# A planner that charges no lag between two operations of one stream on one engine

## The chip, the core and the metric

The kernel runs on one core of one Trainium2 chip. The metric is device time in microseconds (us) of one execution of the whole program. The core has five engines that read their own instruction queues in order: TensorE (PE in the profile; PEld is its weight load), VectorE (DVE), ScalarE (ACT), GpSimd (POOL) and SyncE (SP), which issues most of the transfers.

## The reference, cut to what matters

One encoder block on 256 tokens of width 2048, in float32. One input projection feeds two branches, latent attention and a two-way RWKV-7 scan; both are gated, projected, merged, projected again, normalised and added to the input.

```python
h = rms_norm(x, g_pre)
proj = h @ w_in                      # 2048 x 10688
mla_in, rwkv_in, z_mla, z_rwkv, gate_mla, gate_rwkv = jnp.split(proj, ...)
q = rms_norm(q_a) @ mla_wq_b;  kv = rms_norm(kv_a) @ mla_wkv_b
y_mla = mla_attention(q_nope, rot(q_rope), k_nope, rot(k_rope), v_mla)   # 8 heads, softmax
rin = rin + rwkv_mu * (centred_shift(rin) - rin)
w, a = decay(...), sigmoid(...)      # low-rank, forward and backward
# for each of 256 steps, both directions, 16 heads of 64 x 64:
#   st = st * w_t + (st @ a_t) b_t^T + v_t k_t^T ;  y_t = st @ r_t
y = rwkv7_bidir_scan(r_h, hd(w_f), hd(w_b), k_fh, k_bh, v_h, kk, hd(a_f), hd(a_b))
y_rwkv = group_norm(y) + bonus * v
u_mla  = (y_mla  * silu(z_mla))  @ w_br_mla
u_rwkv = (y_rwkv * silu(z_rwkv)) @ w_br_rwkv
merged = sigmoid(gate_mla) * u_mla + sigmoid(gate_rwkv) * u_rwkv
x = x + rms_norm(merged @ w_out, g_post)
```

## The kernel before, in words

**The main line.** All large products run on PE as three matmuls each: every float32 operand is split into a high part and the rest (hi and lo), and hi x hi, hi x lo and lo x hi are summed in PSUM. The weights come in 249 chunks, most of 512 KB. A chunk is loaded by SyncE into one of three `raw` buffers, ACT writes its high part to one of three `whi` (line 327, reached from the split stream), DVE writes the rest to one of three `wlo` (L330), and PE consumes it: four steps of six matmuls of 256 columns in the input projection (L396 and L397 read `whi`, L398 reads `wlo`). So a split can start only when PE has finished the chunk three places ahead of it, and PE stands still when the next `wlo` is late.

**The side work.** The RWKV heads are handled in four quads of four heads. For each quad: the operands are prepared (`front_k`, `front_v`, `front_d`, `bonus`); PE makes eight groups of Gram products and transposes (L797, L805), which DVE masks out of PSUM into `g` (five banks go round); DVE turns part of them by two long transposes (L818, L819) and inverts 32 x 32 triangles in place, 30 rounds of a multiply into `tmp` and an add into `u` (both at helper line L191), each of which needs the one before it. Then four scan steps alternate between PE (L892 or L912 with L914, then L923, then L941 with L944) and copies on ACT and DVE (L916 and L918, L925 and L927), and a group norm ends the quad (`yr`). This side work has no priority in time of its own; what PE does in between is the main line.

**What sets the order.** The program is written out by a planner, the class `Streams`, while the kernel is built. Every piece of work is a generator (a stream) that asks for an engine (P, A, D, G or S for PE, ACT, DVE, GpSimd, SyncE) with a cost in us and, where it names one, a ready time. After each pick the stream's own time `s[2]` is set to the end of that operation plus `LAG` of the engine: 0.25 us for P, 0.12 for A, D and G, 2.0 for S. The next request of the stream is ready at that time unless it names another. On each engine the planner takes, among requests that could start within `SLOT` (0.08 us on DVE, 0.06 on ACT, 0.03 on PE) of the earliest, the one with the lowest rank. The main matmuls have rank 9. The stream that splits chunks has rank 1 when fewer than two chunks are split ahead of the matmuls, and otherwise 8. The quads' chain (`chunks_of`) has rank 2, `front_k` and `front_d` 3, `bonus` 5, the evictions of Gram products 0. The planner's times are its own and do not reach the chip: only the order of each engine's instructions and their semaphore waits do.

Of the kernel before, what the change touches and what calls it, by code (L numbers as in the profile page):

```python
# [43 lines left out]
class Streams:  # L44
# [11 lines left out]
        self.mode = "128x128"  # L56

    def add(self, gen, rank, t=0.0):
        s = [gen, rank, t, None]
        self.live.append(s)  # L60
        self._next(s, None)
        return s
# [15 lines left out]
    def run(self, until=None):  # L78
        while self.live and not (until and until()):
            moved = True  # L80
            while moved:
                moved = False
                for s in list(self.live):
                    while s in self.live and s[3][0] in "WT" and (s[3][0] == "T" or s[3][1]()):
                        if s[3][0] == "T":
                            s[2] = max(s[2], s[3][1])
                        self._next(s, s[2])
                        moved = True
            if until and until():
                return  # L90
            ask = {}
            for i, s in enumerate(self.live):
                q = s[3]
                if q[0] != "W":
                    ready = s[2] if len(q) < 3 or q[2] is None else q[2]
                    rank = s[1]() if callable(s[1]) else s[1]
                    ask.setdefault(q[0], []).append((max(self.free[q[0]], ready), rank, i, s))
            best = None
            for e, c in ask.items():
                first = min(c)[0] + SLOT[e]  # L100
                start, _, _, s = min((x for x in c if x[0] <= first), key=lambda x: (x[1], x[0], x[2]))
                if best is None or start < best[2]:
                    best = (e, s, start)
            if best is None:
                if not self.live:
                    return
                raise RuntimeError("every stream waits: " + " ".join(self.where(x[0]) for x in self.live))
            _, s, start = best
            e, cost = s[3][0], s[3][1]
            if e == "P":  # L110

                mode = s[3][3] if len(s[3]) > 3 else "128x128"
                cost += 0.2 * (mode != self.mode)
                self.mode = mode
            elif len(s[3]) > 3 and s[3][3] != self.table:
                self.table = s[3][3]
                cost += 1.3
            self.free[e] = start + cost
            self.used[e] += cost
            s[2] = start + cost + self.LAG[e]  # L120
            self._next(s, s[2])
# [1532 lines left out]
```

## Time and profile before

| what | us |
|---|---|
| three timed runs: median, lowest, highest | 875.97, 873.17, 876.22 |
| profiled execution, its own time | 872.72 |
| its span, first to last instruction | 870.9 |
| PE busy (8112 matmuls) | 848.3 |
| DVE busy | 659.3 |
| ACT busy | 501.1 |

The span is 1.8 us shorter than the execution's own time. A matmul's record is longer than its place in the row: records of 0.28 us follow each other every 0.12 us, so that a busy PE is not a PE at its peak, and an idle gap of PE is shown shorter than it is. In a row of the timeline, the bracket at the end gives how long the engine was idle before it and which instruction released it. Names such as `wlo`, `g`, `u`, `yr` are tiles, with the buffer number left out.

### The profile page before, as it was taken

To read this page: it belongs to the slowest core of one execution; us is meant where nothing else is said; L and a number is where in the kernel's file an instruction comes from. 1 tells how busy PE (TensorE), PEld (TensorE's weight loads), DVE (VectorE), ACT (ScalarE), POOL (GpSimd) and SP (SyncE) were. 2 spreads that over 40 slices of the span, in tenths; PEclk is the share of its full clock that TensorE was granted. 3 is DMA by queue.
4 is the path that set the end of the run, shared out by engine and by line. 5 is a ranking of instruction groups with operands and counts; after the bars stand their busy time and mean duration, and the time that the engine had idled before them with its cause. 6 is when DMAs were issued, how large, how long until landed. Compare 5 with 4: busy or idle time off the path is not lost.

```text
span 870.9 us, 19398 instructions
## 1 busy us (share of the span) xinstructions
PE 848.3 (97%) x8112; PEld 810.0 (93%) x8112; DVE 659.3 (76%) x1082; ACT 501.1 (58%) x797; POOL 30.7 (4%) x66
## 2 busy tenths in 40 slices
PE   9999999999999999999999999999999999999996
PEld 8999999988899998999889999899999999998884
DVE  5878898868987878988789878775867556775554
ACT  6777644487544578354776445586766434444442
POOL 4110000000000000000000000000000000000000
PEclk9999999999999999999999999999999999999999
DMA  9565646633376523565423665346444675555553
GB/s 286 169 181 148 176 129 187 169 99 90 101 212 177 161 68 97 158 193 169 132 76 96 195 188 152 98 149 186 136 128 147 232 257 190 176 193 193 194 195 119
DMA packets 123528, 139.41 MB, mean 160 GB/s; under 512 B 6704, under 2 KB 110512, under 8 KB 123056
## 3 DMA queue, kind: packets, MB, share of 16 engines
q1 hardware_dynamic: 121664, 135.16, 52.4%
q0 software_dynamic: 768, 1.57, 0.6%
q10 hardware_dynamic: 1008, 1.44, 0.5%
q8 instruction: 63, 1.03, 0.5%
q14 instruction: 25, 0.20, 0.1%
HBM read 136.05 MB, written 2.10 MB: 159 GB/s over the span
## 4 chain that ended last, share of the span: by engine, by line
PE 73%; DVE 14%; ACT 8%; issue 2%; DMA 2%; DVEq 0%; ACTq 0%
PE d L396 16%; PE d L398 16%; PE d L397 15%; DVE wlo L330 4%; PE m L1334 2%; PE m L1335 2%; PE m L1336 2%; ACT whi L327 2%; DVE work L191 2%; PE m L398 2%; PE m L396 2%; PE m L397 2%; PE d L1335 1%; PE d L1334 1%; PE d L1336 1%
## 5 line engine op out<-in xcount | busy, mean ns | idle before, releaser
L327 ACT CAST whi<-raw 128x1024 fp32r<-128x1024 f32 (+3 forms) x252 | 252.8, 1004 | 254.2 <-PE d L397 155.1
L330 DVE TENSOR_TENSOR wlo<-raw,whi 128x1024 fp32r<-128x1024 f32 (+3 forms) x250 | 292.4, 1171 | 125.0 <-ACT whi L327 123.4
L396 PE MATMUL d<-hhi,whi 128*128 128x256 f32 (+1 forms) x1296 | 375.1, 289 | 0.0
L398 PE MATMUL d<-hhi,wlo 128*128 128x256 f32 (+1 forms) x1296 | 366.5, 283 | 2.3 <-DVE wlo L330 2.3
L397 PE MATMUL d<-hlo,whi 128*128 128x256 f32 (+1 forms) x1296 | 366.2, 283 | 0.0
L396 PEld LDWEIGHTS d<-hhi,whi 128*128 128x128 f32 (+1 forms) x1296 | 246.8, 190 | 4.5
L398 PEld LDWEIGHTS d<-hhi,wlo 128*128 128x128 f32 (+1 forms) x1296 | 246.9, 190 | 2.7 <-DVE wlo L330 2.7
L397 PEld LDWEIGHTS d<-hlo,whi 128*128 128x128 f32 (+1 forms) x1296 | 247.1, 191 | 0.1
L191 DVE TENSOR_TENSOR work<-work,work 128x512 f32<-128x512 f32 (+5 forms) x64 | 38.8, 612 | 3.9 <-ACT work L575 1.2
L191 DVE TENSOR_TENSOR u<-u,tmp 128x30 f32<-128x30 f32 (+7 forms) x120 | 29.9, 250 | 3.0
L191 DVE TENSOR_TENSOR tmp<-u 128x30 f32<-128x30 f32 (+7 forms) x120 | 29.8, 249 | 2.9
L396 PE MATMUL d<-b,whi 128*128 128x256 f32 x96 | 27.1, 282 | 0.0
L398 PE MATMUL d<-b,wlo 128*128 128x256 f32 x96 | 27.1, 282 | 0.0
L398 PE MATMUL d<-ar,wlo 128*128 128x256 f32 x96 | 27.0, 281 | 0.0
L397 PE MATMUL d<-work,whi 128*128 128x256 f32 x96 | 26.9, 280 | 0.0
L397 PE MATMUL d<-ar,whi 128*128 128x256 f32 x96 | 26.9, 280 | 0.0
L396 PE MATMUL d<-ar,whi 128*128 128x256 f32 x96 | 26.8, 279 | 0.0
L1334 PE MATMUL m<-whi,hhi 128*128 128x512 f32 x60 | 23.3, 389 | 0.0
L1335 PE MATMUL m<-wlo,hhi 128*128 128x512 f32 x60 | 23.3, 389 | 0.0
L1336 PE MATMUL m<-whi,hlo 128*128 128x512 f32 x60 | 23.3, 389 | 0.0
L191 DVE TENSOR_TENSOR g<-m,mask 128x512 f32<-128x512 f32 x32 | 20.6, 686 | 0.0
L797 PE MATMUL m<-ar,u 64*128 64x128 f32 x256 | 19.2, 285 | 0.3 <-DVE g L191 0.3
(334 smaller groups left out, 1487.3 us busy)
## 6 DMA issues: line engine op xcount, KB each, us to landing
raw<-in_w_in_dram SPq DMA_DIRECT2D x160, 512.0 KB, 3.9
raw<-in_w_out_dram SPq DMA_DIRECT2D x32, 512.0 KB, 3.6
raw<-in_w_br_mla_dram SPq DMA_DIRECT2D x16, 512.0 KB, 4.0
raw<-in_w_br_rwkv_dram SPq DMA_DIRECT2D x16, 512.0 KB, 3.3
raw<-in_mla_wkv_b_dram SPq DMA_DIRECT2D x8, 512.0 KB, 3.9
raw<-in_mla_wq_b_dram SPq DMA_DIRECT2D x8, 384.0 KB, 3.3
raw<-in_w_in_dram SPq DMA_DIRECT2D x7, 384.0 KB, 5.3
g<-in_x_dram SPq DMA_DIRECT2D x2, 1024.0 KB, 6.9
```

What stands on the lines that cost most here:

```text
L191: dve.tensor_tensor(out=o, in0=a, in1=b, op=op)
L327: act.copy(dst(c.hi), src(raw))
L330: eng.tensor_tensor(out=dst(c.lo), in0=src(raw), in1=dst(c.hi).bitcast(F32), op=ALU.subtract)
L396: pe.matmul(o, hi[:, c:c + m], xhi(k), start=k == k_first and i % 2 == 0, stop=False)
L397: pe.matmul(o, hi[:, c:c + m], xlo(k), start=False, stop=False)
L398: pe.matmul(o, lo[:, c:c + m], xhi(k), start=False, stop=last)
L797: pe.matmul(m[:, q * 128:q * 128 + 128], z.kb[R64[h], d, j, q], z.ar[d][R64[h], j, q], start=q == 0, stop=q == 3)
L1334: pe.matmul(banks[t], hhi[:, k, T], hi, start=k == 0, stop=False)
L1335: pe.matmul(banks[t], hhi[:, k, T], lo, start=False, stop=False)
L1336: pe.matmul(banks[t], hlo[:, k, T], hi, start=False, stop=k == KT - 1)
```

## The change

A stream's record gets a fifth field, the engine of its last operation. When the stream's next request is for the same engine and its ready time is the stream's own time, the lag is taken off again: the planner then treats the next operation as ready the moment the last one ends, whether or not it reads what the last one wrote. A request for another engine keeps the lag. Nothing else is edited, and both programs hold the same instructions on every engine: 7026 on PE, 1080 on DVE, 778 on ACT by the builder's count; PE also changes between its tile shapes 140 times in each.

```diff
     def add(self, gen, rank, t=0.0):
-        s = [gen, rank, t, None]
+        s = [gen, rank, t, None, ""]
...
                 if q[0] != "W":
                     ready = s[2] if len(q) < 3 or q[2] is None else q[2]
+                    if s[4] == q[0] and ready == s[2]:
+
+                        ready -= self.LAG[q[0]]
                     rank = s[1]() if callable(s[1]) else s[1]
...
             _, s, start = best
             e, cost = s[3][0], s[3][1]
+            s[4] = e
```

What it moves is seen in the order of the instructions. Line numbers of the changed kernel are higher by 4.

DVE, first quad, start of the inversion (`tmp` and `u`), behind its second transpose; `wlo` rows are chunk splits, `work` rows with `qpad` or `d` evict a projection. Before:

```order
132 L330 TENSOR_TENSOR wlo_22_84<-raw_16_78,whi_19_81 128x1024
133 L191 TENSOR_TENSOR tmp_1365<-u_81_1364 128x30
134 L191 TENSOR_TENSOR u_81_1364<-u_81_1364,tmp_1365 128x30
135 L191 TENSOR_TENSOR tmp_1365<-u_81_1364 128x29
136 L330 TENSOR_TENSOR wlo_23_85<-raw_17_79,whi_20_82 128x1024
137 L191 TENSOR_TENSOR work_25_87<-qpad_51_121 128x512
138 L191 TENSOR_TENSOR u_81_1364<-u_81_1364,tmp_1365 128x29
139 L194 SCALAR_TENSOR_TENSOR work_28_90<-d_112,iv_66,work_25_87 128x256
140 L191 TENSOR_TENSOR tmp_1365<-u_81_1364 128x56
141 L194 SCALAR_TENSOR_TENSOR work_28_90<-d_112,iv_66,work_25_87 128x256
142 L191 TENSOR_TENSOR u_81_1364<-u_81_1364,tmp_1365 128x28x2
143 L330 TENSOR_TENSOR wlo_21_83<-raw_15_77,whi_18_80 128x1024
```

Now:

```order
127 L334 TENSOR_TENSOR wlo_23_85<-raw_17_79,whi_20_82 128x1024
128 L195 TENSOR_TENSOR tmp_1272<-u_81_1271 128x29
129 L195 TENSOR_TENSOR u_81_1271<-u_81_1271,tmp_1272 128x29
130 L195 TENSOR_TENSOR tmp_1272<-u_81_1271 128x56
131 L195 TENSOR_TENSOR u_81_1271<-u_81_1271,tmp_1272 128x28x2
132 L195 TENSOR_TENSOR tmp_1272<-u_81_1271 128x54
133 L195 TENSOR_TENSOR u_81_1271<-u_81_1271,tmp_1272 128x27x2
134 L195 TENSOR_TENSOR tmp_1272<-u_81_1271 128x78
135 L334 TENSOR_TENSOR wlo_21_83<-raw_15_77,whi_18_80 128x1024
136 L195 TENSOR_TENSOR u_81_1271<-u_81_1271,tmp_1272 128x26x3
```

Rounds of the inversion stand next to each other, seven instructions between two splits, where other work stood between them.

DVE, fourth quad, the end of the Gram products (`g`) and the two transposes; `yr` rows are the group norm of the third quad. Before:

```order
637 L330 TENSOR_TENSOR wlo_22_84<-raw_16_78,whi_19_81 128x1024
638 L191 TENSOR_TENSOR yr_113<-yr_113,work_196_5489 128x512
639 L191 TENSOR_TENSOR g_198_5523<-m_106,mask_63 128x512
640 L191 TENSOR_TENSOR g_198_5523<-m_105,mask_63 128x512
641 L194 SCALAR_TENSOR_TENSOR yr_113<-yr_113,iv_66,work_26_88 128x256 x2
642 L191 TENSOR_TENSOR yr_113<-yr_113,work_37_99 128x512
643 L818 STREAM_TRANSPOSE u_204_5657<-g_198_5523 32x1024
644 L819 STREAM_TRANSPOSE u_204_5657<-g_198_5523 32x1024
645 L330 TENSOR_TENSOR wlo_23_85<-raw_17_79,whi_20_82 128x1024
```

Now:

```order
623 L334 TENSOR_TENSOR wlo_23_85<-raw_17_79,whi_20_82 128x1024
624 L195 TENSOR_TENSOR g_198_5492<-m_108,mask_63 128x512
625 L195 TENSOR_TENSOR g_198_5492<-m_106,mask_63 128x512
626 L822 STREAM_TRANSPOSE u_204_5578<-g_198_5492 32x1024
627 L823 STREAM_TRANSPOSE u_204_5578<-g_198_5492 32x1024
628 L198 SCALAR_TENSOR_TENSOR work_25_87<-work_109_2439,d_110 128x512
629 L334 TENSOR_TENSOR wlo_21_83<-raw_15_77,whi_18_80 128x1024
```

The group norm of the quad before has moved ahead of this place, and one split stands right in front of the last two evictions.

PE, third quad, the first scan step: L892 opens it, L923 needs the copy of its result, and what stands between covers that copy (L684 to L686 are a low-rank product, L587 and L588 head sums). Before:

```order
3069 L892 MATMUL m_105<-uv_3970,g_157_4061 64x64 x8
3070 L684 MATMUL m_108<-tw_45_115,work_165_5000 128x256
3071 L685 MATMUL m_108<-tw_46_116,work_165_5000 128x256
...
3075 L686 MATMUL m_108<-tw_45_115,work_166_5001 128x256
3076 L923 MATMUL m_105<-work_161_4195,g_157_4061 64x64 x8
```

Now:

```order
2924 L896 MATMUL m_109<-uv_3775,g_157_4038 64x64 x8
2925 L688 MATMUL m_107<-tw_45_115,work_165_4834 128x256
...
2931 L591 MATMUL m_106<-work_167_4846,bdr_68 128x256
...
2935 L400 MATMUL d_111<-hhi_75,whi_19_81 128x256
...
2940 L402 MATMUL d_111<-hhi_75,wlo_22_84 128x256
2941 L927 MATMUL m_109<-work_61_806,g_157_4038 64x64 x8
```

Between the two, 6 matmuls stood before and 16 stand now.

## Rows read from the trace of the kernel before

**Rows 1.** Page, part 1: engines' busy us, share of the span, instructions.

```profile
PE 848.3 (97%) x8112; PEld 810.0 (93%) x8112; DVE 659.3 (76%) x1082; ACT 501.1 (58%) x797; POOL 30.7 (4%) x66
```

**Rows 2.** Timeline of PE, two matmuls of the main line: start, us, instruction.

```profile
239.15 0.28 PE L396 MATMUL d<-hhi,whi 128*128 128x256 f32 x1
239.27 0.28 PE L397 MATMUL d<-hlo,whi 128*128 128x256 f32 x1
```

**Rows 3.** Stretches: length; busy PE, PEld, DVE, ACT, POOL (instructions); clock, DMA share, GB/s.

```profile
90.00:150.00 60.00, 60.00 (x525) 58.97 (x524) 52.03 (x91) 29.65 (x39) 1.13 (x3) 1.00 0.58 162
210.00:240.00 30.00, 28.59 (x258) 26.96 (x256) 29.59 (x41) 20.84 (x31) 1.02 (x2) 1.00 0.34 96
450.00:480.00 30.00, 28.92 (x264) 27.50 (x262) 28.31 (x40) 22.07 (x34) 0.00 (x0) 1.00 0.32 89
```

**Rows 4.** Waits of PE: who, for whom: us in total, times, longest.

```profile
PE m L923 <- DVE work L918: 3.1, 8, 0.7
PE d L398 <- DVE wlo L330: 2.3, 2, 1.2
PE m L587 <- ACT work L435: 1.3, 2, 0.7
PE m L588 <- DVE work L191: 1.2, 5, 0.3
PE m L1414 <- POOL ones L250: 1.1, 1, 1.1
...
PE m L1203 <- ACT work L1194: 0.2, 1, 0.2
```

**Rows 5.** Timeline of DVE in the first quad's inversion.

```profile
120.51 0.21 DVE L191 TENSOR_TENSOR tmp<-u 128x30 f32<-128x30 f32 x1
120.75 0.21 DVE L191 TENSOR_TENSOR u<-u,tmp 128x30 f32<-128x30 f32 x1
...
123.30 0.21 DVE L191 TENSOR_TENSOR u<-u,tmp 128x29 f32<-128x29 f32 x1
123.42 0.48 DVE L194 SCALAR_TENSOR_TENSOR work<-d,iv,work 128x256 f32<-128x256 f32 x1
...
141.72 1.23 DVE L330 TENSOR_TENSOR wlo<-raw,whi 128x1024 fp32r<-128x1024 f32 x1 [0.49 <-ACT whi L327]
```

**Rows 6.** Waits of all engines, the two that hold the splits.

```profile
ACT whi L327 <- PE d L397: 155.1, 102, 2.2
DVE wlo L330 <- ACT whi L327: 123.4, 136, 5.5
```

**Rows 7.** Timeline of DVE, then PE: second quad's masks, transposes, splits; what waited.

```profile
227.16 1.23 DVE L330 TENSOR_TENSOR wlo<-raw,whi 128x1024 fp32r<-128x1024 f32 x1
228.29 1.29 DVE L191 TENSOR_TENSOR g<-m,mask 128x512 f32<-128x512 f32 x2
...
235.60 2.02 DVE L819 STREAM_TRANSPOSE u<-g 32x1024 f32<-32x1024 f32 x1
237.65 2.36 DVE L330 TENSOR_TENSOR wlo<-raw,whi 128x1024 fp32r<-128x1024 f32 x2
...
238.93 0.39 PE L398 MATMUL d<-hhi,wlo 128*128 128x256 f32 x1 [1.25 <-DVE wlo L330]
```

**Rows 8.** The same place in the fourth quad.

```profile
470.03 1.23 DVE L330 TENSOR_TENSOR wlo<-raw,whi 128x1024 fp32r<-128x1024 f32 x1
...
478.70 2.36 DVE L330 TENSOR_TENSOR wlo<-raw,whi 128x1024 fp32r<-128x1024 f32 x2
...
479.99 0.39 PE L398 MATMUL d<-hhi,wlo 128*128 128x256 f32 x1 [1.05 <-DVE wlo L330]
```

**Rows 9.** Timeline of PE: one Gram group and one transpose group, first quad.

```profile
101.58 1.16 PE L797 MATMUL m<-ar,u 64*128 64x128 f32 x16
...
103.49 0.60 PE L805 MATMUL m<-iv,u 128*128 128x128 f32 x4
```

**Rows 10.** Timeline of PE, third quad's first scan step, ahead of L923.

```profile
424.11 0.68 PE L923 MATMUL m<-work,g 64*64 64x64 f32 x16 [0.72 <-DVE work L918]
```

## The prediction

> **What bounds the kernel now.** I read the busy table first [rows 1]: PE is busy 97% of the span. Since matmul records overlap, I looked at their pitch: two matmuls of the main line start 0.12 us apart while each record lasts 0.28 [rows 2]. So the main line runs at one matmul per 0.12 us, and a chunk of 24 takes 2.9 us. Next the table by stretches [rows 3]. The granted clock is 1.00 in each, the upper of the two levels, so nothing is to be won there. Where a quad's Gram products meet the group norm of the quad before (210 to 240 and 450 to 480), DVE is busy 29.6 and 28.3 us of 30 and PE misses 1.4 and 1.1. In the inversion (90 to 150) DVE is busy 87%, yet PE misses nothing. PE bounds the kernel; for moments, DVE does.
>
> So a change of order can touch only what PE waits. The list of its waits of over 0.15 us has 15 groups, from 3.1 to 0.2 us, with a sum of 13.8; the five largest and the last are shown [rows 4]. The first matmul's 1.1 us and 1.5 us of the input's transposes (L1465) belong to the start, before the main line flows, and stay. That leaves 11.2 us in some 27 cases. A wait also hides the tail of the record before it, 0.28 - 0.12 = 0.16 us, 4.3 us for 27. The stake is 15.5 us, 1.8% of the time, if every wait went. On the losing side there is no such limit.
>
> **The change part by part.**
>
> *What moves.* Nothing is added or removed, and PE changes its tile shape as often as before, so PE's own work is the same. Three things move. Gram products and transposes, requests of one stream on one engine, close up on PE. Operations that a stream has in a row on DVE or ACT close up too. And the chunk splits lose against them by rank until fewer than two chunks are in hand: of the 143 splits that the planner gives out between the 40th and the 600th of the 944 main-line steps, 32 had the urgent rank before and 100 have it now.
>
> *Late splits.* What do they cost in the inversions? A split turns urgent when the last step of a chunk is given out; PE then has that step (6 x 0.12 = 0.7 us) and the next chunk (2.9 us) in hand, 3.6 us. The split needs at most the short instruction in front of it, about 0.3 us, and its own 1.23 [rows 5], 1.5 us. Its `whi` is mostly there: in the trace ACT waits 155 us for PE to free a `whi`, and DVE waits 123 us for ACT behind that [rows 6], so splits so far stood ready too early, with DVE idle (0.49 us at 141.7) [rows 5]. About 2 us of cover remain, and I cost this at nothing. If the cover is gone, a late split costs PE what the two cases in the trace cost, 1.0 to 1.3 us [rows 7, 8]; rival D is built on that.
>
> *Starvation at the Gram products.* From the end of the split at 227.2 to the start of the next at 237.65, DVE does 9.3 us of masks, group norm and transposes, and PE waits 1.25 us for `wlo` [rows 7]. From 471.3 to 478.7 it does 7.4 us, and PE waits 1.05 [rows 8]. With their hidden tails these two cost 2.6 us. In the new order the fourth quad has only two masks and two transposes behind its last split, 2 x 0.65 + 2 x 2.02 = 5.3 us [rows 7]. By the measure of the old order, where 7.4 us brought 1.05, that brings none: -1.2. In the second quad the group norm of the first still stands among the masks: 18 instructions of some 10 us, a split, then 4.0 us of transposes. Its eight PE groups, four of 1.2 us and four of 0.6 [rows 9], now stand in a row without a main-line step, at most 7 us that need no split but do need the masks to empty PSUM. I keep the old 1.4 us there (bounds 0 to 3). In such a row each mask of 0.65 us is waited for sooner; I add 0.6 us for the first two quads, in whose rows no main-line step is left (bounds 0 to 2). Term: -1.2 + 0 + 0.6 = -0.6 us, bounds -2.6 to +3.
>
> *The scan steps.* PE waits ahead of L923 3.1 us in 8 cases [rows 4], 4.4 with tails. Covered by six matmuls it waits 0.72 us [rows 10]. Over the 16 scan steps 174 other matmuls stood ahead of L923; now 215 do, 16 of them at the place just named. Ahead of L941 and L944 there were 182 and are 177, with five places of only six in place of two. 41 x 0.12 = 4.9 us of cover are new, but most of it stands where there was no wait. I take half of the 4.4 us as gained and 0.5 us as lost ahead of L941: -1.7 us, bounds -4 to +2.
>
> *Neighbours that depend on each other.* An instruction behind one that it needs starts 0.24 us after it (120.51, 120.75); one behind an equally short one that it does not need starts 0.12 us after it (123.30, 123.42) [rows 5]. So the lag of 0.12 us was right for dependent neighbours and wrong for independent ones; the change does half of what it says. In the order, DVE instructions that read what the one in front wrote go from 236 to 306. 70 x 0.12 = 8.4 us of DVE time are unknown to the new plan. 23 of the 70 are rounds of the inversion, whose planned cost has a pad of 0.115 us anyway, and some 15 are softmax steps behind the last quad. About 30 lie in the dense stretches, 3.6 us, and PE sees them only where it waits for DVE at that moment: I take a fifth, +0.7 us, bounds 0 to +3.6.
>
> The rule on this is in the Trainium skill, page "VectorE: DVE Perf Modes", section "The DRAIN you can't avoid": behind every DVE operation the pipe empties before the next one starts, and a semaphore between two adds nothing. By it all neighbours cost the same, this term would be 0 and the sum 0.7 us lower. The trace disagrees with 0.24 against 0.12 us; the section itself adds that a next operation that is not held starts earlier.
>
> *Head sums.* L587 and L588 wait 2.5 us for ACT and DVE [rows 4]. Nothing in the change aims at them: 0, bounds -2 to +2.
>
> *Sum.* -0.6 - 1.7 + 0.7 + 0 = -1.6 us: 872.7 us of the profiled execution become 871.1. That execution was 3.3 us under the median of the timed runs; carried over, 875.97 becomes 874.4. The three timed runs differ by 3 us, twice the gain.
>
> **The rivals.**
>
> *A, the forecast:* PE's waits shrink by 0.5 to 4 us: 874.4.
>
> *B, the waits only change places:* what is won in the fourth quad is lost in the second and at the masks. For it: a quad's DVE work is the same, and both orders are packed on the same estimates. Against: the inversions have room that was not used. 876.
>
> *C, a deeper gain:* chains of a quad get shorter, since a dependent operation no longer stands behind a 1.23 us split, and scan steps are better covered. If half of the 15.5 us goes: 868.2. For it: 215 matmuls for 174. Against: the chains are hidden behind PE anyway, so that a shorter one alone gives nothing.
>
> *D, slower:* splits are now last-minute, and DVE runs late against its plan by the dependent neighbours. It decides at 2 us: where DVE is that much behind when a split turns urgent, PE waits. A quad has about 8 unplanned neighbours in dense stretches, 1 us. If two places in each quad fall through at 1.0 to 1.3 us, 8 x 1.15 = 9.2 us are lost; less the 1.6 gained, +7.6: 883.6. For it: 100 urgent splits. Against: the 2 us.
>
> That the edit does nothing is excluded for the order and is B for the time.
>
> **How the numbers follow.** A 0.42, B 0.25, C 0.14, D 0.19. A change of 0.5%, 4.4 us, is about what a measurement of this kernel can tell from none. Faster by more: most of C and a little of A, 0.22. Slower by more: most of D, 0.18. Within: 0.60. The range leaves out the far half of C and the far half of D: 868.5 to 882.5.
>
> **What would show it.** Right: L398's wait for `wlo` gone in the fourth quad; L923's wait under 2 us; no gap of PE in the inversions although DVE's 123 us ahead of `wlo` have shrunk; the new row of Gram groups with short waits for `g`. Wrong towards D: waits of L398 of 0.3 to 1.3 us inside inversions or scan steps. Wrong towards B: waits of L398 at the transposes of other quads, or more than 1 us at L797 and L805. If PE waits under 6 us in all behind the start, C was right.

## The result, and the profile after

The changed kernel takes 880.37 us (median of 5 runs, 880.26 to 883.29), the kernel before 875.81 (5 runs on the same chip, 872.94 to 876.22). The medians differ by 4.6 us. The ratio, which is taken over all runs, is 1.0074 with a 95% interval of 1.0048 to 1.0099, some 6.5 us: slower, and over the 0.5% that a measurement tells from no change. The prediction was 874.4. The time lies in its range, but the sign is the other one.

The profiled execution after took 883.29 us with a span of 881.5; that of before 872.72 and 870.9. So the two traces differ by 10.5 us, more than the medians: the trace of after is of its slowest run and that of before of a fast one. 3.1 of the 10.5 us arise in the first 35 us, and the first experiment shows them to be no property of the order. This leaves 7.4 us to explain in the traces.

The page, part 1, of after, answering to [rows 1]: busy times are the same within 3 us, and what grew is idle time.

```profile
PE 851.0 (97%) x8112; PEld 810.7 (92%) x8112; DVE 662.3 (75%) x1082; ACT 501.2 (57%) x797; POOL 30.5 (3%) x66
```

The waits of PE in after (in total, times, longest), answering to [rows 4]; all lines stand 4 higher than before.

```profile
PE m L927 <- DVE work L922: 4.3, 8, 0.8
PE m L1491 <- DVE work L201: 2.4, 1, 2.4
PE m L801 <- DVE g L195: 2.0, 3, 0.9
PE m L809 <- DVE g L195: 1.9, 3, 0.9
...
PE d L402 <- DVE wlo L334: 1.6, 2, 1.2
PE m L1207 <- DVE work L201: 1.4, 4, 0.6
...
PE m L1021 <- DVE work L195: 0.8, 1, 0.8
```

Three of these were small or absent before: the Gram products and transposes (L801, L809) wait for DVE to mask earlier ones out of PSUM (`g`), and the softmax transposes (L1207) wait for DVE. The wait of L1491 belongs to the start.

A table by place in us, worked out from all starts on PE behind 30 us: the distance of two starts less the pitch of that tile shape, wherever PE idled in between (so tails are in it).

| place | before | after | difference |
|---|---|---|---|
| Gram rows (L797, L805 before; L801, L809 after) | 0.5 | 5.8 | +5.3 |
| `wlo` (L398; L402) | 2.6 | 2.5 | -0.1 |
| softmax (L1203; L1207) | 0.9 | 3.3 | +2.4 |
| scan steps (L862, L912, L923, L941) | 8.4 | 9.2 | +0.8 |
| head sums (L587, L588) | 5.0 | 3.1 | -1.9 |
| `front_v`, `front_d` (L648, L686) | 1.5 | 0.7 | -0.8 |
| L1017; L1021 | 0 | 1.0 | +1.0 |
| sum | 18.9 | 25.6 | +6.7 |

The sum accounts for 6.7 of the 7.4 us. The wait at L1021 (sums of the norms on the latent branch) and the gains at head sums and fronts belong to none of the three places. The stretches of after, answering to [rows 3], and the inversions of the four quads (same columns):

```profile
90.00:150.00 60.00, 59.16 (x511) 57.58 (x511) 55.15 (x107) 28.66 (x38) 1.14 (x3) 1.00 0.55 152
210.00:240.00 30.00, 27.71 (x254) 26.24 (x252) 28.45 (x49) 16.91 (x24) 1.02 (x2) 1.00 0.47 136
450.00:480.00 30.00, 28.60 (x259) 27.25 (x259) 29.68 (x40) 17.43 (x23) 0.00 (x0) 1.00 0.46 126
120.00:150.00 30.00, 30.00 (x253) 30.00 (x252) 28.04 (x72) 12.50 (x15) 0.12 (x1) 1.00 0.68 186
240.00:270.00 30.00, 30.00 (x253) 30.00 (x252) 28.33 (x66) 13.73 (x15) 0.12 (x1) 1.00 0.65 182
360.00:390.00 30.00, 30.00 (x253) 30.00 (x252) 27.81 (x67) 13.29 (x16) 0.00 (x0) 1.00 0.67 190
480.00:510.00 30.00, 30.00 (x253) 30.00 (x252) 27.62 (x74) 13.14 (x15) 0.00 (x0) 1.00 0.68 193
```

PE is busy all through the four inversions although splits are late there: the loss isn't rival D's. It sits in the dense stretches. The fourth quad's Gram row in the trace of after, PE and then DVE:

```profile
461.56 1.16 PE L801 MATMUL m<-ar,u 64*128 64x128 f32 x16
462.65 0.66 PE L809 MATMUL m<-iv,u 128*128 128x128 f32 x4
463.24 1.16 PE L801 MATMUL m<-ar,u 64*128 64x128 f32 x16
464.86 0.66 PE L809 MATMUL m<-iv,u 128*128 128x128 f32 x4 [0.46 <-DVE g L195]
...
467.58 1.16 PE L801 MATMUL m<-ar,u 64*128 64x128 f32 x14 [0.94 <-DVE g L195]
...
463.71 0.49 DVE L198 SCALAR_TENSOR_TENSOR work<-work,iv,work 128x256 f32<-128x256 f32 x1
464.12 1.28 DVE L195 TENSOR_TENSOR g<-m,mask 128x512 f32<-128x512 f32 x2
465.31 0.48 DVE L198 SCALAR_TENSOR_TENSOR work<-work,iv,work 128x256 f32<-128x256 f32 x1
465.71 1.22 DVE L334 TENSOR_TENSOR wlo<-raw,whi 128x1024 fp32r<-128x1024 f32 x1
466.84 1.28 DVE L195 TENSOR_TENSOR g<-m,mask 128x512 f32<-128x512 f32 x2
```

The same groups before, each with six main-line matmuls behind it, which are left out here:

```profile
460.49 1.16 PE L797 MATMUL m<-ar,u 64*128 64x128 f32 x16
...
462.40 0.60 PE L805 MATMUL m<-iv,u 128*128 128x128 f32 x4
...
463.64 1.16 PE L797 MATMUL m<-ar,u 64*128 64x128 f32 x16
```

A second Gram group now starts 1.68 us behind the first (461.56, 463.24); before, 3.15 us lay between them. The masks come no sooner, with a split and a `bonus` operation among them, and PE stands until a mask has emptied a bank: the transposes at 464.86 start behind the first mask of the pair at 464.12, the matmuls at 467.58 behind the first of the pair at 466.84.

### The profile page after: what moved, and what is told of

Same layout as the page of the kernel before. It is cut to its first block, busy times and chain, and to the rows that moved or that the text cites. A ratio compares the mean times of both kernels' runs of the same rounds, so it can differ in the third digit from the quotient of the medians.

```text
span 881.5 us, 19391 instructions
## 1 busy us (share of the span) xinstructions
PE 851.0 (97%) x8112; PEld 810.7 (92%) x8112; DVE 662.3 (75%) x1082; ACT 501.2 (57%) x797; POOL 30.5 (3%) x66
## 4 chain that ended last, share of the span: by engine, by line
PE 64%; DVE 18%; ACT 12%; issue 3%; DMA 2%; SPq 0%; DVEq 0%; ACTq 0%
PE d L400 13%; PE d L402 13%; PE d L401 13%; DVE wlo L334 5%; DVE work L195 2%; PE m L1340 2%; PE m L1339 2%; PE m L1338 2%; ACT whi L331 2%; DVE work L198 1%; PE m L402 1%; PE m L400 1%; PE m L401 1%; PE d L1339 1%; PE d L1340 1%
## 5 line engine op out<-in xcount | busy, mean ns | idle before, releaser
L402 PE MATMUL d<-hhi,wlo 128*128 128x256 f32 (+1 forms) x1296 | 367.1, 283 | 1.8 <-DVE wlo L334 1.6
L402 PEld LDWEIGHTS d<-hhi,wlo 128*128 128x128 f32 (+1 forms) x1296 | 247.1, 191 | 2.7 <-DVE wlo L334 2.7
L402 PE MATMUL d<-b,wlo 128*128 128x256 f32 x96 | 27.1, 282 | 0.0
L402 PE MATMUL d<-ar,wlo 128*128 128x256 f32 x96 | 26.9, 280 | 0.0
L801 PE MATMUL m<-ar,u 64*128 64x128 f32 x256 | 20.8, 286 | 2.1 <-DVE g L195 2.0
L801 PEld LDWEIGHTS m<-ar,u 64*128 64x128 f32 x256 | 17.0, 187 | 5.3 <-DVE g L195 3.0
```

Source lines behind the costliest of these rows:

```text
L402: pe.matmul(o, lo[:, c:c + m], xhi(k), start=False, stop=last)
L801: pe.matmul(m[:, q * 128:q * 128 + 128], z.kb[R64[h], d, j, q], z.ar[d][R64[h], j, q], start=q == 0, stop=q == 3)
```

## Experiments: where the loss sits

Two theories, S and R in the expectations. **S**: the loss is made at definite places; from the trace of after I had the start, the Gram rows and the softmax. **R**: any order other than the one before costs about this much, wherever it differs. The kernels were timed in five groups, each against runs of before of its own, whose medians were 874.33, 873.59, 873.76, 873.88 and 873.63 us. A ratio is taken over all runs, so it is not quite that of the medians. Unless said otherwise an edit is one to the condition that the change adds:

```
if s[4] == q[0] and ready == s[2]:
    ready -= self.LAG[q[0]]
```

**The start, and the rest.** The rule in the first 32 us of the plan alone:

```
-if s[4] == q[0] and ready == s[2]:
+if s[4] == q[0] and ready == s[2] and self.free["P"] < 32.0:
```

> The lag is taken off only while the planner's PE clock is under 32 us, so the start is ordered as in the changed kernel and the planner then goes on by the old rule. Theory S (the loss has places: about 3 us in the start, where PE now waits for the matmul of line L1491 at 21.6 us; about 3 to 5 us at the Gram products; about 2 us in the softmax steps): 2 to 4 us above the kernel before, 878 to 880, with the wait of PE for DVE ahead of L1491 of about 2.4 us. Theory R (any order other than the one that the kernel's constants were chosen for is worse, wherever it differs): slower by some other amount, with waits spread over the quads and no single one of 2 us.

Measured 873.43, ratio 0.9991 (0.9982 to 1.0000). And behind the start alone (`>= 32.0`):

> The lag is taken off only once the planner's PE clock has passed 32 us: the start is that of the kernel before. Theory S: the changed kernel's time less 3 us, 876.5 to 878.5, with waits of L801 and L809 for g of 3 us or more. Theory R: as slow as the changed kernel, 879 to 882.

Measured 879.53, ratio 1.0060 (1.0047 to 1.0072). So all of the loss is made behind the start, and S loses the 3 us that it had there; by the number alone R was right here. Its trace repeats the waits of after (Gram rows 5.8, softmax 3.2 in the table's measure).

**By engine.** The rule on PE alone (`and q[0] == "P"`), then on ACT and DVE alone (`and q[0] in "AD"`):

> The lag is taken off on PE alone. Theory S: Gram products and transposes close up, waits of L801 and L809 for g of 3 to 5 us, nothing in the start and none in the softmax: 878 to 881. Theory R: no closer to the changed kernel than to the kernel before; 874 to 882. If the Gram rows cost nothing by themselves: 875 to 877.

> The lag is taken off on DVE and ACT, and kept on PE. Theory S: the start costs its 3 us and the softmax 2, the Gram products keep main-line steps between them and wait under 1.5 us: 878 to 881. Theory R: 876 to 884, with Gram waits as in the changed kernel or elsewhere.

Measured 881.64, ratio 1.0080 (1.0067 to 1.0093), and 880.17, ratio 1.0059 (1.0044 to 1.0074). Each half costs as much as the whole, which at this point spoke for R. But the places differ: the softmax costs 0.9 us with PE's half, as before, and 3.2 with the other, while Gram rows and `wlo` together cost 7.7 and 5.3 against 3.1 before.

**Controls without the rule.** The kernel before, with the planner's numbers moved by amounts that mean nothing on the chip:

```
-    return 0.08 + 1.04e-3 * n
+    return 0.081 + 1.04e-3 * n
```

> The kernel before with no change of rule: only the planner's base cost of a DVE operation is 0.081 instead of 0.08 us, a thousandth of a microsecond that is true of nothing on the chip, but which tips ties and so reorders most of the program. Theory R (the loss is the price of any reordering: the order before happens to be a lucky one among many that the estimates can't tell apart): 3 to 9 us slower than before, with new waits of PE for wlo, for the masks and in the scan steps at other places than before. Theory S (the loss is made by what the change aims at, the closed-up Gram rows and softmax steps): within 2 us of before, 872 to 877 us, with some 21 us of PE's gaps as before.

```
-    return 0.1 + 0.83e-3 * n + 0.09 * aps
+    return 0.105 + 0.83e-3 * n + 0.09 * aps
```

> The same sort of control on another engine: the planner's base cost of an ACT operation is 0.105 instead of 0.1 us, nothing else. R: 3 to 9 us slower than before. S: within 2 us of before.

Then `LAG` at 0.11 for A and D, and at 0.24 for P:

> The kernel before with its lag on ACT and DVE at 0.11 instead of 0.12 us everywhere; the rule of the change isn't in it. R: 3 to 9 us slower than before, like the two controls of cost. S: within 2 us of before; if it is faster, a shorter lag as such helps.

> The kernel before with its lag on PE at 0.24 instead of 0.25 us; this reorders about a quarter as many instructions as the other controls. R: 0 to 5 us slower than before, in proportion to what it reorders. S: within 2 us of before.

Measured 886.63, 874.86, 873.32 and 873.17 us; ratios 1.0147 (1.0134 to 1.0161), 1.0017 (1.0008 to 1.0027), 1.0004 (0.9989 to 1.0018) and 0.9993 (0.9982 to 1.0004). Counted in the programs as built, the places of PE, DVE and ACT that hold another instruction than before are 54%, 42%, 46% and 14% in these four, and 60% in the changed kernel; the fourth has mostly other buffers at the same places and the waits of before, so it tests little. R as put falls: the second and the third move nearly half of the program and cost 1.3 us and nothing. But a thousandth of a microsecond on DVE's price costs 13 us, so S's "within 2 us" falls too: an order can be bad by accident. What happened there is told under the hardware. A single pair of kernels further down can therefore not exclude luck; places in the traces that move as expected weigh more than times.

**By stream.** The rule behind the start, without the attention heads (`and s[0].__name__ != "head"`), then without the stream of Gram products and inversion (`!= "chunks_of"`), then without both:

> The changed rule behind the start, but the attention heads keep the lag; to be read against the run with the rule everywhere behind the start (879.53 us). Theory S (the loss is made at definite places: Gram rows, softmax transposes): the heads' neighbours on DVE are dependent, the plan had them 0.12 us too early, PE came too early to L1207; with the lag back the six waits of 0.3 to 0.8 us between 622 and 664 us go, and 2.2 us with them: 877.3 us. In the milestones the excess over before stays what it is up to 600 us (+5) and doesn't grow behind it. Theory R (luck of the order): the time is 873 to 887 us with new waits at other places, since the order behind an early difference is another one throughout.

> The changed rule behind the start, but the stream that issues the Gram products, their transposes, the inversion and the first part of a quad's chain keeps the lag; to be read against 879.53 us. S: the waits at the Gram products and their transposes (L801, L809: 5.8 us with tails) fall to 1.5 us, those for wlo return to the 2.6 of before, the softmax waits stay: 876 us. R: no relation of place and edit; 873 to 887 us.

> The rule behind the start, in all streams but that one and the attention heads. If the two places are all of the loss: 877.3 less 2 us, 875 us, at most 1.5 us over before, and no place left where the excess over before grows by more than 1 us. If something else loses too, or another order costs by itself: 877 us or more.

Measured 878.9, 877.33 and 875.87 us; ratios 1.0051 (1.0035 to 1.0066), 1.0039 (1.0024 to 1.0054) and 1.0027 (1.0015 to 1.0039). The medians are 1.6, 1.3 and 0.9 us above what S expected. The traces are sharper than the medians. The start of the k-th matmul of the main line, against the trace of before:

| k (its start before, us) | 144 (31.8) | 1600 (252.2) | 2400 (379.3) | 3200 (506.7) | 3700 (583.6) | 4400 (688.0) |
|---|---|---|---|---|---|---|
| rule behind the start | +1.1 | +0.2 | +1.3 | +3.1 | +5.3 | +7.5 |
| without the heads | +1.0 | +0.1 | +1.2 | +3.1 | +5.2 | +5.4 |
| without `chunks_of` | -0.1 | -1.0 | -0.1 | -0.5 | +1.4 | +3.1 |
| without both | +1.7 | +0.8 | +1.7 | +1.3 | +3.1 | +3.3 |

With the lag back in the heads the trace is the same up to 583 us and then grows by 0.2 in place of 2.2 us. With the lag back in `chunks_of` nothing is lost up to 507 us, behind the Gram rows of all four quads, and the softmax loses its 1.7. Each of these two parts of the loss goes with its stream, as S has it. In the medians the heads' part is only 0.6 us (879.53 to 878.9), within the spread of the runs. Without both streams 2.0 us stay, more than the 1.5 expected; in the trace 1.8 us arise between 507 and 584 us, in the last steps of the fourth quad. The rule behind the start loses 2.2 us there as well (5.3 less 3.1), about 1 of them ahead of L1021, and so does the kernel before with one price changed (the second run of the next part, 1.9 to 4.1), but not the rule on PE alone (8.4 to 8.5). That third part is left unexplained. The table also shows that the Gram rows are not a plain sum: when all four are past, at 507 us, the excess of the rule has grown by 2.0 us only, since part of what they lose is won back at the head sums and the fronts.

**Why the Gram rows lose.** One number of the plan can be held against the trace. The planner prices four Gram transposes at 0.72 us and a change of tile shape at 0.2, so that a pair of groups that close up takes 0.9 + 0.72 + 0.4 = 2.02 us in the plan; the trace has 1.68. The planner's own start times, printed while it wrote the program, give the rest (us; PE's first group of a quad is set to its planned time):

| quad | before: from one Gram group to the next | masks, late against the plan | after: from one to the next | masks, late |
|---|---|---|---|---|
| 1 | 3.1, 3.2, 2.9 | -1.1 to 0 | 1.7, 2.3, 2.3 | 0.4 to 0.6 |
| 2 | 3.2, 3.2, 3.2 | 0.1 to 0.3 | 1.7, 1.9, 2.8 | 0.9 to 1.3 |
| 3 | 3.2, 3.2, 3.2 | 0.1 to 0.5 | 1.7, 2.4, 3.0 | 0.1 to 0.6 |
| 4 | 3.2, 2.9, 3.2 | -0.2 | 1.7, 2.9, 3.1 | 0.9 to 1.1 |

The distances are those of the trace; a pair that closes up is planned at 2.02. So PE runs 0.34 us ahead of its plan with each pair that closes up, and DVE up to 1.3 us behind it. Before, PE ran ahead too, by 0.30 us with each step (3.15 against a planned 3.45), and hardly waited: the old lag of 0.25 us made room for a main-line step between the groups, and on this reading for both errors. Now the price mended, in the changed kernel and in the kernel before:

```
-                e = yield ("P", 0.72)
+                e = yield ("P", 0.4)
```

> The changed kernel with one more edit: the planner's price of a group of four Gram transposes is 0.40 instead of 0.72 us (the trace has 0.35 to 0.6). S with the reason that PE comes to the masks earlier than the plan has it: the plan then knows that PE is early and puts main-line steps in between; the waits at L801 and L809 fall from 3.9 us to under 2, and the time from 880.4 to 877 to 878.5. If the waits stay, it isn't the price of the transposes. R: anything from 873 to 887 us.

> The kernel before with that price alone (0.40 instead of 0.72 us). S: its Gram rows waited 0.5 us in all, so there is little to win: 872 to 875 us. R: like any reordering, 873 to 887 us, with a third of the orders over 876.

Measured 876.53, ratio 1.0034 (1.0021 to 1.0047), and 872.97, ratio 0.9990 (0.9979 to 1.0001). The changed kernel gets about half of its loss back (1.0074 to 1.0034). But its L801 and L809 still wait 3.5 us in the profiled execution, not under 2, one of them for 1.92 us; that execution, 880.01 us, is the slowest of twelve, and eight of them lie between 875.5 and 877.6. So the time came, but not in the waits that were to bring it.

The price together with the lag back in the heads:

> The changed kernel with two edits: the price of a group of Gram transposes at 0.40 us, and the lag kept in the attention heads. If the two places add up: the 876.5 us of the price alone less the 2 us of the softmax waits, 874.5 us (873 where the clock stays at its upper level throughout), as before. If they don't, 876 us or more with waits at other places. The six waits of L1207 (2.9 us with tails) go.

Measured 874.15, ratio 1.0011 (1.0001 to 1.0020), as expected of two places that add up; one wait of 0.6 us at L1207 stayed. Then the two halves within `chunks_of`, without the new price: the lag kept on its PE requests alone, and on its DVE and ACT requests alone.

> The rule behind the start; in the Gram and inversion stream PE's neighbours keep the lag of 0.25 us, DVE's and ACT's don't. To be read against 879.5 us (rule everywhere behind the start) and 877.3 (this stream left out). If PE's closing up makes the loss: main-line steps stand between the Gram groups again, L801 and L809 wait under 1.5 us, 877.3 us. If DVE's and ACT's does: 879 to 880 us, waits as there.

> The counterpart: in that stream DVE's and ACT's neighbours keep the lag, PE's don't. If PE's closing up makes the loss: 879 to 881 us with L801 and L809 at 4 to 6 us with tails in all. If DVE's and ACT's does: 877.3 us.

Measured 880.15, ratio 1.0075 (1.0062 to 1.0088), and 879.77, ratio 1.0066 (1.0054 to 1.0078). With the lag kept on either half alone, the lost time does not come back. In the first, Gram rows and `wlo` cost 2.1 and 3.2 us, in the second 4.4 and 1.2, where the whole rule has 5.8 and 2.2. It looks as if DVE's dense stretch were short of time, and what isn't waited for at the masks were waited for at `wlo`; no run tests that by itself. The question that stayed was whether a closed row loses by itself, since DVE can't supply it, or because the plan misjudges it. PE's half, the one with the largest loss there, with the price mended tells that:

> The rule for neighbours on PE alone (881.6 us in its run, with masks within 0.5 us of their planned times but PE up to 1 us ahead of its own), with the price of a group of Gram transposes at 0.40 instead of 0.72 us. If the mis-estimate makes the loss: PE's gaps in the Gram rows and for wlo fall from 7.7 to about 4 us and the time to 876 us or less. If a closed row as such makes it: they stay at 6 to 8 us and the time over 879 us.

> The changed kernel with that price, the lag kept on DVE and ACT where neighbours mostly depend on each other (the inversion stream and the attention heads); elsewhere, and on PE everywhere, the rule stands. If mis-estimates make the loss: no worse than before, 872.5 to 874.5 us, with the masks within 0.6 us of their planned times, L801, L809 and wlo together under 4 us, and L1207 under 1.5. If closed rows do: 876 us or more.

The second has this condition, and the price:

```
+if s[4] == q[0] and ready == s[2] and not (s[0].__name__ in ("chunks_of", "head") and s[4] != "P"):
```

Measured 874.91, ratio 1.0007 (0.9997 to 1.0018), and 874.71, ratio 1.0011 (1.0001 to 1.0022). PE's waits with PE's half of the rule, first with the old price and then with the new:

```profile
PE d L402 <- DVE wlo L334: 4.6, 3, 2.2
...
PE m L801 <- DVE g L195: 1.4, 1, 1.4
...
PE m L809 <- DVE g L195: 0.4, 1, 0.4
```

```profile
PE d L402 <- DVE wlo L334: 2.3, 2, 1.9
...
PE m L809 <- DVE g L195: 0.4, 1, 0.4
PE m L801 <- DVE g L195: 0.4, 1, 0.4
```

With tails, 7.7 us became 4.2, and the ratio fell from 1.0080 to 1.0007. Of the twelve distances between Gram groups nine are still planned without a gap (1.70 us) and three are wider; in the trace they are 1.7 to 3.2 us. Part of the gain is the clock, which fell twice in the trace with the old price (below) and not in that with the new one. Waits and time came as expected if the mis-estimate makes the loss, so in that kernel the wrong price is the likely cause, and closed rows need not lose; three of the rows did open, and it is one pair of kernels. In the last kernel the time came back, 0.2 us over what was expected, but Gram rows and `wlo` cost 6.8 us in its trace, not under 4, and its masks are up to 1.0 us late. How the lost time is divided between PE too early and DVE too late in the full change stays open, and so does what makes DVE late. No version beat the kernel before measurably: the best, the price alone, has a ratio of 0.9990 with an interval that includes 1.

## Why the prediction was wrong, step by step

The terms summed to -1.6 us, and the places in the traces to +6.7. In the prediction's order:

- **Late splits, 0 us: right.** ACT's wait for PE to free a `whi` fell from 155 to 146 us and DVE's ahead of `wlo` from 123 to 114 [rows 6], and the inversions show no gap of PE. Rival D got the sign, and with +7.6 us came nearer than the forecast. Its premise that DVE falls behind its plan shows in the masks (up to 1.3 us), but the late splits that were to cost the time didn't occur.

```profile
ACT whi L331 <- PE d L401: 146.0, 103, 2.7
...
DVE wlo L334 <- ACT whi L331: 113.8, 95, 5.4
```

- **Starvation at the Gram products, -0.6 (bounds -2.6 to +3): the step that failed.** It measured +5.2, outside its bounds: the Gram rows +5.3, `wlo` -0.1. Of its parts, the fourth quad's gain came (no wait for `wlo` there any more, [rows 8]), and the second quad kept its own:

```profile
227.42 0.39 PE L402 MATMUL d<-hhi,wlo 128*128 128x256 f32 x1 [1.24 <-DVE wlo L334]
```

  What was mis-sized is the 0.6 us for masks that are waited for sooner. I gave it to the first two quads, because the order there has no main-line step left in the row, and used no duration against the plan. The rows had what was needed: a group of 1.16 us and one of 0.60 [rows 9] against planned 0.9 and 0.72 with 0.2 for each change of shape. Closing such a row takes away the step that hid the difference, in all four quads. How much of the 5.3 us is this price and how much is DVE's lateness stays open. The prediction's own sign for B came, more than 1 us at L797 and L805: they waited 3.9 us (L801 and L809 after).

- **Scan steps, -1.7 (bounds -4 to +2): measured +0.8.** L923's own gaps went from 5.1 to 6.3 us, though 215 in place of 174 matmuls stood ahead of it. Counting cover said where PE has work, not when DVE delivers; of the eight waits [rows 4] none went in number. What made them longer isn't shown.

- **Dependent neighbours, +0.7 (bounds 0 to +3.6): the size was off, and the place.** The softmax alone gives +2.4. The prediction saw some 15 such neighbours behind the last quad and set them aside. There the rest of DVE isn't dense, but PE has a transpose waiting at the end of each short chain. In the trace of after:

```profile
625.74 0.44 PE L1207 MATMUL m<-iv,work 128*128 128x128 f32 x2 [0.45 <-DVE work L201]
...
630.83 0.41 PE L1207 MATMUL m<-iv,work 128*128 128x128 f32 x2 [0.32 <-ACT work L1198]
...
631.81 0.41 PE L1207 MATMUL m<-iv,work 128*128 128x128 f32 x2 [0.57 <-DVE work L201]
...
635.74 0.41 PE L1207 MATMUL m<-iv,work 128*128 128x128 f32 x2 [0.27 <-DVE work L201]
```

  Keeping the lag in the heads left one wait of 0.7 us of these, and it comes with DVE's and ACT's half of the rule, not with PE's.

- **Head sums, 0 (within 2): measured -1.9**, at the edge of its bounds. Nothing was foreseen at L1021 (+1.0) and at the fronts (-0.8).

## What to carry to other kernels

In a kernel whose order is planned from estimated times, a pad that is wrong by itself may cover another estimate that is wrong the other way. Before taking it out, hold each price of the rows that will close up against the trace, and mend those first: here 0.72 in place of 0.40 us for one kind of group went with about half of the 0.7%. And before reading a change of order by its mechanism, time a few orders that differ for no reason, and see that they do differ; of four, one was nearly that of before, two lay within 0.2% of it and one at 1.5%.

## What the runs showed of the hardware

A wait of PE can cost more than its length, since the granted clock can fall behind it from 1.00 to 0.5 (2.4 to 1.2 GHz) for some microseconds. In the control at 886.63 us PE waited 2.57 and 1.91 us close together, and the stretches read (columns as in [rows 3]):

```profile
583.99 1.16 PE L944 MATMUL m<-g,uv 128*64 128x64 f32 x16 [2.57 <-ACT uv L925]
587.06 0.58 PE L587 MATMUL m<-work,bdr 128*128 128x256 f32 x1 [1.91 <-ACT work L435]
...
580.00:585.00 5.00, 2.37 (x38) 1.99 (x36) 2.08 (x3) 3.51 (x5) 0.19 (x1) 0.83 0.24 78
585.00:590.00 5.00, 2.95 (x15) 2.50 (x12) 3.28 (x5) 2.47 (x6) 0.00 (x0) 0.50 0.19 69
590.00:595.00 5.00, 5.00 (x31) 5.00 (x30) 1.59 (x4) 2.11 (x4) 0.00 (x0) 0.64 0.00 0
```

In that trace it fell at two other places too, around waits of 2.09 and 2.01 us. Whether it falls behind a wait of a given length is not settled by the wait. Two kernels have the same wait of 2.25 us for `wlo` in the second quad, the one with the rule on DVE and ACT alone and the one with the lag kept on PE in `chunks_of`. In the first trace the clock stayed, in the second it fell:

```profile
231.24 0.38 PE L402 MATMUL d<-hhi,wlo 128*128 128x256 f32 x1 [2.25 <-DVE wlo L334]
...
230.00:235.00 5.00, 3.76 (x31) 3.76 (x32) 4.89 (x7) 2.61 (x3) 0.00 (x0) 1.00 0.51 140
```

```profile
229.04 0.38 PE L402 MATMUL d<-hhi,wlo 128*128 128x256 f32 x1 [2.25 <-DVE wlo L334]
...
225.00:230.00 5.00, 2.75 (x20) 2.54 (x20) 4.96 (x4) 2.21 (x3) 0.00 (x0) 0.93 0.00 0
230.00:235.00 5.00, 5.00 (x34) 5.00 (x33) 4.55 (x13) 1.50 (x2) 0.00 (x0) 0.73 0.90 264
```

The changed kernel with the mended price shows the cost: its seven executions with a mean clock of 0.997 or 0.998 took 875.5 to 877.6 us, the four with 0.993 to 0.995 took 878.7 to 880.0. In the one that was traced (880.0) the clock fell behind the wait of 1.92 us; if it was that wait in the others too, it is worth some 3 us more in a part of the executions. The kernel with the rule on PE alone ran at 0.992 to 0.994 in all its runs; in its trace the clock fell behind a wait of 2.23 us and again behind one of 1.36.

A long wait isn't needed. In the run with the new price and the lag kept in the heads the clock fell in a scan step of the first quad, behind low-rank products and head sums, with gaps of PE of 0.34 and 0.45 us among them:

```profile
169.60 1.03 PE L927 MATMUL m<-work,g 64*64 64x64 f32 x16 [0.45 <-DVE work L922]
...
165.00:170.00 5.00, 4.21 (x44) 3.21 (x43) 2.91 (x6) 4.56 (x9) 1.01 (x2) 0.97 0.73 213
170.00:175.00 5.00, 5.00 (x54) 4.66 (x54) 2.33 (x5) 4.03 (x5) 0.00 (x0) 0.50 0.38 109
```

In the first 800 us of the trace of after the clock fell once, in the start, behind the 2.4 us of L1491; behind the start its waits are 1.24 us at most, and the clock stays at 1.00.
